# A two-layer hybrid encoder trunk: large products as one plain float32 matmul in place of three float32r matmuls on split operands

## The chip, the cores and the metric

The kernel runs on one core of one Trainium2 chip. The metric is the device time of one execution in microseconds (us), the median of several runs. TensorE (PE in the profile) multiplies matrices, VectorE (DVE), ScalarE (ACT) and GpSimd (POOL) work elementwise, and SyncE (SP) issues all DMAs of this kernel in order. PEld is TensorE's weight load.

## The reference

The input x has 512 tokens of width 1024, in float32. Two layers each do

```
x += 0.5 * SwiGLU(RMSNorm(x))            # 1024 -> 2 x 2816 -> 1024
x += W_out( sum_m sigmoid(gate_m) * P_m(mixer_m(RMSNorm(x))) )
x += 0.5 * SwiGLU(RMSNorm(x))
```

The four mixers read one common input projection of the normalised x (10520 columns): differential attention, gated linear attention (GLA), a Mamba-2 state space (SSD), and RWKV-7, which is a recurrence over the tokens. A last RMSNorm gives the output. All weights are float32 and are read once: 478 blocks ("units") of 128 x 1024 numbers, 512 KB each.

## The kernel before

**Units and products.** `unit` loads 128 x 1024 weights, copies them on ScalarE into a float32r tile `whi` and takes the rest `wlo = wraw - whi` on VectorE. (float32r is a matmul input type of four bytes and of less precision than float32.) The other operand of each large product stands as such a pair too: `xh/xl` after a norm, `hh/hl` after the gated product of a feed-forward block (FFN), `yh/yl` and `ah/al` in the merge. `mm3` then makes a product of three matmuls:

```
mm(out=ps, lhsT=lh, rhs=rh, start=first, stop=False)
mm(out=ps, lhsT=lh, rhs=rl, start=False, stop=False)
return mm(out=ps, lhsT=ll, rhs=rh, start=False, stop=last)
```

In what follows a *product* is one such step: 128 x 128 stationary numbers times 128 x 512 moving ones into one PSUM tile. A unit makes eight. `feat` makes 128 features of all tokens (eight products), `tok` makes 512 columns for four token tiles, `merge` multiplies a branch by its slice of the branch weights. `feat2` makes the first two units of an FFN or mixer with 256 moving columns at a time, because the second half of the tokens is normalised later.

**Stages.** Each layer is FFN, mixer, FFN. An FFN is 44 units of gate and up projection and 22 of the down projection. A mixer has 59 `feat` units (32 of them the gates), 24 `tok` units, 16 merge units and 8 of the output projection.

**The order in the mixer.** `cotrace` writes two streams of work, RWKV (`first`) and the three other branches (`others`), in the order of estimated times that they yield (TensorE's cost of a piece, and the latency after it). Where TensorE would idle, it puts in a piece of a `filler`: first the 32 gate units, then the merges. Merges come only after RWKV and attention are done. A scheduler in the framework then orders the instructions of each engine; each engine runs its list in order.

RWKV's chain per half of its heads is: projections and preparation; a triangular inverse on VectorE of 62 small instructions (tiles `itmp` and `xi`), which goes through DRAM before and after (`nx<-nd`, `xdi<-xi`) and ends in the matmuls of lines 705 and 709; then eight chunks in turn, each a chain of matmuls (lines 735, 743, 749, and 759 and 762 for the output) with small VectorE work between; then the store of the branch. Narrow matmuls of the mixers (transposes, attention, chunks) take plain float32 operands already.

Of the kernel before, what the change touches and what calls it, by code (L numbers as in the profile page):

```python
# [11 lines left out]
F32R = mybir.dt.float32r  # L12
# [61 lines left out]
class Body:  # L74
# [4 lines left out]
    # ---------------------------------------------------------------- helpers  # L79
# [22 lines left out]
    def rsqrt(self, y, a, pool, tag):  # L102
        """y = a ** -0.5 for normal positive a."""
# [14 lines left out]
    def rsqrt_neg_half(self, hm, pool):  # L118
        """a ** -0.5 for the [128, 1] tile hm = -a / 2."""
# [3 lines left out]
        # the shifted sign and the halved exponent are in the constant  # L123
# [38 lines left out]
    def mm3(self, ps, lh, ll, rh, rl, first, last):  # L162
        mm = self.nc.tensor.matmul
        mm(out=ps, lhsT=lh, rhs=rh, start=first, stop=False)  # L164
        mm(out=ps, lhsT=lh, rhs=rl, start=False, stop=False)  # L165
        return mm(out=ps, lhsT=ll, rhs=rh, start=False, stop=last)  # L166

    def feat(self, ap):
        """[128 features, 512 tokens] of the projection by one unit."""
        hi, low = self.unit(ap)  # L170
        ps = self.small("pb")
        for k in range(8):
            c = slice(k * 128, (k + 1) * 128)
            self.mm3(ps, hi[:, c], low[:, c], self.xh[:, k, :], self.xl[:, k, :], k == 0, k == 7)
        return ps

    def feat2(self, aps):
        """Two units' projections, the first half of the tokens before the second."""
        ws = [self.unit(ap, "pool") for ap in aps]
        pss = [self.small("pb") for _ in aps]  # L180
        last = None
        for h in range(2):
            n = slice(256 * h, 256 * h + 256)
            for (hi, low), ps in zip(ws, pss):
                for k in range(8):
                    c = slice(k * 128, (k + 1) * 128)
                    last = self.chained(last if k == 0 else None, lambda: self.mm3(
                        ps[:, n], hi[:, c], low[:, c], self.xh[:, k, n], self.xl[:, k, n], k == 0, k == 7))
        return pss

    def tok(self, units, lh, ll, tags=("pb", "pb", "oy", "oy"), tail=0):
        """Four [128 tokens, 512] products: stationary lh/ll (feature-major), moving the units.
        The last tail units go by token tile, so that the tiles end one after another."""
        mm = self.nc.tensor.matmul
# [3 lines left out]
        def one(t, k, hi, low):  # L198
            lt = slice(t * 128, (t + 1) * 128)
            c = slice((k % 2) * 512, (k % 2 + 1) * 512)  # L200
            mm(out=pst[t], lhsT=lh(k)[:, lt], rhs=hi[:, c], start=k == 0, stop=False)  # L201
            mm(out=pst[t], lhsT=lh(k)[:, lt], rhs=low[:, c], start=False, stop=False)  # L202
            mm(out=pst[t], lhsT=ll(k)[:, lt], rhs=hi[:, c], start=False, stop=k == nk - 1)  # L203

        n = len(units) - tail
        for u, ap in enumerate(units[:n]):
            w = self.unit(ap)
            for k in (2 * u, 2 * u + 1):
                for t in range(NT):
                    one(t, k, *w)  # L210
        ws = [self.unit(ap) for ap in units[n:]]
        for t in range(NT):
            for j, w in enumerate(ws):
                for k in (2 * (n + j), 2 * (n + j) + 1):
                    one(t, k, *w)
# [5 lines left out]
    # ------------------------------------------------------------------ norm  # L221
# [9 lines left out]
    def norm_(self, x, gain, pool, out=None, g=None):  # L231
        """RMS norm of x (tiles [t][half]); to xh/xl feature-major, or rows to out."""
        nc = self.nc
        if out is None:
            self.xh = self.xp.tile([128, 8, 512], F32R, tag="xh", name="xh")
            self.xl = self.xp.tile([128, 8, 512], F32R, tag="xl", name="xl")
        if g is None:
            g = self.gain_row(gain, pool)
        for t in range(NT):
            # hm = -(mean square + eps) / 2, the first half's part ahead of the second's  # L240
# [8 lines left out]
            for h in range(2):  # L249
# [8 lines left out]
                nc.scalar.copy(self.xh[o], ps)  # L258
                self.sub(self.xl[o], ps, self.xh[o].bitcast(F32))
# [1082 lines left out]
```

## Time and profile before

| | |
|---|---|
| median of 3 runs | 3218.39 us (3214.93 to 3223.4) |
| span of the profiled execution | 3212.2 us |
| PE busy | 3147.8 us |
| DVE busy | 1621.3 us |
| ACT busy | 1148.1 us |
| moved by DMA | 338.50 MB, mean 105 GB/s |

The profiled execution is listed with its span only; the median of the runs lies 6.2 us (0.2%) above it. Busy time of PE is a sum over overlapping matmuls, whose ends are modelled, so the rate of the matmuls is read from their starts.

### The profile page before, as it was taken

The page shows a single profiled execution, that of the slowest core. Times are in us where ns is not written, and L with a number is a line of the kernel's source. Part 1 is how long each engine was busy: PE and PEld are TensorE (multiplying, and loading weights), DVE is VectorE, ACT ScalarE, POOL GpSimd, SP SyncE. Part 2 cuts the span into 40 slices and gives each one's busy share as a digit, 9 for nine tenths or more (in the row PEclk, how much of TensorE's full clock was granted, in tenths as well). Part 3 has the DMA queues.
Part 4 walks back from the last instruction along what each step waited for, and adds up shares of the span by engine and source line. Part 5 has one row for each costly group of instructions (what it writes and reads, how often), then busy time and mean ns, then how long its engine had stood idle before and what let it go on. Part 6 is the DMA issues. An engine that isn't in the chain of part 4 may idle for free.

```text
span 3212.2 us, 40884 instructions
## 1 busy us (share of the span) xinstructions
PE 3147.8 (98%) x16160; PEld 2499.3 (78%) x16160; DVE 1621.3 (50%) x3310; ACT 1148.1 (36%) x1754; POOL 137.8 (4%) x160
## 2 busy tenths in 40 slices
PE   8999999999999999999999999999999999999998
PEld 6888787777777777888888888777777777778887
DVE  4332446756475775332343324567654757753323
ACT  3222245654432323222222223356553323232222
POOL 0000000000011100000000000000000011000000
PEclk9999999999999999999999999999999999999999
DMA  4222322322222543222332233223122215432222
GB/s 165 98 98 93 129 89 88 103 67 96 86 83 63 180 168 138 99 98 93 108 132 94 99 112 110 93 87 104 60 93 95 86 56 181 172 132 93 98 99 79
DMA packets 138592, 338.50 MB, mean 105 GB/s; under 512 B 35104, under 2 KB 43680, under 8 KB 137632
## 3 DMA queue, kind: packets, MB, share of 16 engines
q1 hardware_dynamic: 138400, 335.88, 30.8%
q8 instruction: 127, 2.08, 0.3%
q14 instruction: 65, 0.53, 0.1%
HBM read 297.55 MB, written 38.27 MB: 105 GB/s over the span
## 4 chain that ended last, share of the span: by engine, by line
PE 90%; DVE 7%; ACT 2%; issue 1%; DMA 0%; SPq 0%; DVEq 0%; ACTq 0%
PE pb L164 18%; PE pb L165 18%; PE pb L166 18%; PE oy L203 3%; PE oy L201 3%; PE oy L202 3%; PE pb L202 2%; PE pb L201 2%; PE pb L203 2%; PE rs L203 1%; PE os L203 1%; PE rs L201 1%; PE os L201 1%; PE os L202 1%; PE rs L202 1%; PE os L871 1%
## 5 line engine op out<-in xcount | busy, mean ns | idle before, releaser
L157 ACT CAST whi<-wraw 128x1024 fp32r<-128x1024 f32 x478 | 501.6, 1051 | 1479.6 <-PE pb L165 545.8
L159 DVE TENSOR_TENSOR wlo<-wraw,whi 128x1024 fp32r<-128x1024 f32 x466 | 571.7, 1227 | 894.5 <-ACT whi L157 880.8
L164 PE MATMUL pb<-xh,whi 128*128 128x512 f32 (+1 forms) x2448 | 957.0, 391 | 4.9 <-DVE rwr L97 2.7
L165 PE MATMUL pb<-xl,whi 128*128 128x512 f32 (+1 forms) x2448 | 949.5, 388 | 3.4 <-DVE xl L81 3.4
L166 PE MATMUL pb<-xh,wlo 128*128 128x512 f32 (+1 forms) x2448 | 949.6, 388 | 0.0
L164 PEld LDWEIGHTS pb<-xh,whi 128*128 128x128 f32 x2448 | 466.5, 191 | 110.2 <-issue 16.6
L165 PEld LDWEIGHTS pb<-xl,whi 128*128 128x128 f32 x2448 | 466.7, 191 | 95.8 <-issue 6.3
L166 PEld LDWEIGHTS pb<-xh,wlo 128*128 128x128 f32 x2448 | 467.0, 191 | 93.5 <-issue 6.1
L81 DVE TENSOR_TENSOR s<-s,pb 128x512 f32<-128x512 f32 x88 | 60.5, 688 | 286.9 <-PE pb L166 284.8
L100 ACT ACT_TABLE_LOAD x118 | 151.4, 1283 | 12.5 <-PE os L1141 9.7
L165 PE MATMUL pb<-yl,whi 128*128 128x512 f32 x256 | 102.1, 399 | 0.9 <-DVE yl L81 0.9
L164 PE MATMUL pb<-yh,whi 128*128 128x512 f32 x256 | 102.5, 403 | 0.0
L166 PE MATMUL pb<-yh,wlo 128*128 128x512 f32 x256 | 102.1, 399 | 0.0
L159 POOL TENSOR_TENSOR wlo<-wraw,whi 128x1024 fp32r<-128x1024 f32 x12 | 28.4, 2379 | 1318.3 <-ACT whi L157 1318.3
L202 PE MATMUL pb<-wlo,xh 128*128 128x512 f32 x192 | 76.7, 399 | 0.0
L201 PE MATMUL pb<-whi,xh 128*128 128x512 f32 x192 | 76.6, 399 | 0.0
L201 PE MATMUL oy<-whi,xh 128*128 128x512 f32 x192 | 76.0, 396 | 0.0
L203 PE MATMUL oy<-whi,xl 128*128 128x512 f32 x192 | 75.8, 395 | 0.0
L203 PE MATMUL pb<-whi,xl 128*128 128x512 f32 x192 | 75.8, 395 | 0.0
L202 PE MATMUL oy<-wlo,xh 128*128 128x512 f32 x192 | 75.3, 392 | 0.0
L201 PE MATMUL pb<-whi,hh 128*128 128x512 f32 x176 | 69.1, 392 | 0.0
L202 PE MATMUL pb<-wlo,hh 128*128 128x512 f32 x176 | 69.0, 392 | 0.0
(418 smaller groups left out, 4339.7 us busy)
## 6 DMA issues: line engine op xcount, KB each, us to landing
wraw<-in_ffn_gu SPq DMA_DIRECT2D x176, 512.0 KB, 3.2
wraw<-in_win_f SPq DMA_DIRECT2D x118, 512.0 KB, 3.3
wraw<-in_ffn_d SPq DMA_DIRECT2D x88, 512.0 KB, 3.2
wraw<-in_win_t SPq DMA_DIRECT2D x48, 512.0 KB, 3.3
gd<-sg SPq DMA_DIRECT2D x64, 256.0 KB, 2.1
wraw<-in_wbr SPq DMA_DIRECT2D x32, 512.0 KB, 3.4
msg<-gd SPq DMA_DIRECT2D x64, 256.0 KB, 3.0
wraw<-in_wout SPq DMA_DIRECT2D x16, 512.0 KB, 3.2
```

The costliest lines, as they stand in the source:

```text
L81: return (eng or self.nc.vector).tensor_tensor(out=out, in0=in0, in1=in1, op=op)
L100: return self.nc.scalar.activation(out=out, in_=in_, func=func, **kw)
L157: nc.scalar.copy(hi, raw)
L159: eng.tensor_tensor(out=low, in0=raw, in1=hi.bitcast(F32), op=ALU.subtract)
L164: mm(out=ps, lhsT=lh, rhs=rh, start=first, stop=False)
L165: mm(out=ps, lhsT=lh, rhs=rl, start=False, stop=False)
L166: return mm(out=ps, lhsT=ll, rhs=rh, start=False, stop=last)
L201: mm(out=pst[t], lhsT=lh(k)[:, lt], rhs=hi[:, c], start=k == 0, stop=False)
L202: mm(out=pst[t], lhsT=lh(k)[:, lt], rhs=low[:, c], start=False, stop=False)
L203: mm(out=pst[t], lhsT=ll(k)[:, lt], rhs=hi[:, c], start=False, stop=k == nk - 1)
L871: mm(out=s[:, 0:n], lhsT=qT[qb][cp_, h, :], rhs=kT[h][cp_, 0:n], start=True, stop=True)
```

## The change

The split is taken out everywhere. A unit is used as it was loaded, the other operands are single float32 tiles (`xT`, `hT`, `y`, the merged `acc`), and each product is one matmul on float32 operands. The casts to float32r and the subtractions go, on weights and on the other operands. Two smaller sums that used float32r pairs (RWKV's `bones` product and the SSD's `gtbd` product) become one float32 matmul each. The weight pool has 8 buffers of one tile instead of 3 of three. `cotrace`'s estimate of a `feat` unit goes from 5.2 to 3.5 and of a `tok` group from 20.8 to 14.0, so the order of the mixer is another one. Comments were dropped.

```diff
-    def unit(self, ap, lo="dve"):
-        nc = self.nc
-        raw = self.wp.tile([128, 1024], F32, tag="wraw", name="wraw")
-        nc.sync.dma_start(out=raw, in_=ap)
-        hi = self.wp.tile([128, 1024], F32R, tag="whi", name="whi")
-        low = self.wp.tile([128, 1024], F32R, tag="wlo", name="wlo")
-        nc.scalar.copy(hi, raw)
-        eng = nc.gpsimd if lo == "pool" else nc.vector
-        eng.tensor_tensor(out=low, in0=raw, in1=hi.bitcast(F32), op=ALU.subtract)
-        return hi, low
+    def unit(self, ap):
+        w = self.wp.tile([128, 1024], F32, tag="w", name="w")
+        self.nc.sync.dma_start(out=w, in_=ap)
+        return w
...
-            self.mm3(ps, hi[:, c], low[:, c], self.xh[:, k, :], self.xl[:, k, :], k == 0, k == 7)
+            self.nc.tensor.matmul(out=ps, lhsT=w[:, k * 128 : (k + 1) * 128], rhs=self.xT[:, k, :],
+                                  start=k == 0, stop=k == 7)
...
-                nc.scalar.copy(self.xh[o], ps)
-                self.sub(self.xl[o], ps, self.xh[o].bitcast(F32))
+                nc.scalar.copy(self.xT[o], ps)
...
-                self.mul(s, s, psu)
-                nc.scalar.copy(hh[:, f, :], s)
-                self.sub(hl[:, f, :], s, hh[:, f, :].bitcast(F32))
+                self.mul(hT[:, f, :], s, psu)
...
-                pe += 5.2
+                pe += 3.5
...
-                mm(out=psb, lhsT=self.bones, rhs=qh, start=True, stop=False)
-                mm(out=psb, lhsT=self.bones, rhs=ql, start=False, stop=True)
+                mm(out=psb, lhsT=self.c("bones"), rhs=q, start=True, stop=True)
...
-            self.wp = ep(name="w", bufs=3)
+            self.wp = ep(name="w", bufs=8)
```

Two places in TensorE's list show what moves. The first is the start of the program, where `feat2` stands between the transposes of the first norm (`os<-ident,xn`). Before:

```order
L256 MATMUL os<-ident,xn 128x128 x16
L164 MATMUL pb<-xh,whi 128x256
L165 MATMUL pb<-xl,whi 128x256
L166 MATMUL pb<-xh,wlo 128x256
L164 MATMUL pb<-xh,whi 128x256
```

With the change, up to the end of the first gate and up projections:

```order
L239 MATMUL os<-ident,xn 128x128 x16
L174 MATMUL pb<-xT,w 128x256 x3
L239 MATMUL os<-ident,xn 128x128 x8
L174 MATMUL pb<-xT,w 128x256 x3
L239 MATMUL os<-ident,xn 128x128 x8
L174 MATMUL pb<-xT,w 128x256 x26
L160 MATMUL pb<-xT,w 128x512 x336
```

Where three matmuls stood for a product there is one, of the same columns.

The second place is the scan of RWKV's second half of heads, at its fifth chunk of eight (`rs<-st,ar` reads the state and begins a chunk, `rs<-un,tt` and `rs<-sav,bk` are its next two steps). Before, the products of an SSD projection (`pb` and `oy`, from `wlo` and `whi`) stand between the steps of the chunk:

```order
L735 MATMUL rs<-st,ar 64x64 x3
L202 MATMUL pb<-wlo,xh 128x512
L203 MATMUL pb<-whi,xl 128x512
L201 MATMUL oy<-whi,xh 128x512
L202 MATMUL oy<-wlo,xh 128x512
L743 MATMUL rs<-un,tt 64x64 x4
L203 MATMUL oy<-whi,xl 128x512
L201 MATMUL oy<-whi,xh 128x512
L202 MATMUL oy<-wlo,xh 128x512
L203 MATMUL oy<-whi,xl 128x512
L749 MATMUL rs<-sav,bk 64x64 x4
```

With the change the same chunk steps (now lines 693, 701 and 707) have only narrow matmuls of the SSD and of RWKV's output between them:

```order
L693 MATMUL rs<-st,ar 64x64 x4
L677 MATMUL rs<-ident,yc 64x64 x4
L1077 MATMUL os<-ident,conv 128x128 x3
L701 MATMUL rs<-un,tt 64x64 x4
L1077 MATMUL os<-ident,conv 128x128
L1085 MATMUL os<-ident,conv 128x128 x2
L707 MATMUL rs<-sav,bk 64x64 x4
```

The products that stood here have moved ahead in the list, and from this chunk to the first merge none is left.

## Rows read from the trace of the kernel before

**Rows 1.** The page: span, busy time by engine, TensorE's granted clock in 40 slices.
```profile
span 3212.2 us, 40884 instructions
PE 3147.8 (98%) x16160; PEld 2499.3 (78%) x16160; DVE 1621.3 (50%) x3310; ACT 1148.1 (36%) x1754; POOL 137.8 (4%) x160
PEclk9999999999999999999999999999999999999999
```
**Rows 2.** Stretches by window: the first layer's mixer; 100 us inside an FFN.
```profile
370.00:1235.00 865.00, 852.38 (x4826) 648.66 (x4825) 551.55 (x1328) 372.61 (x617) 60.07 (x75) 0.99 0.31 104
...
100.00:200.00 100.00, 100.00 (x442) 82.78 (x442) 35.27 (x38) 29.88 (x38) 0.00 (x0) 1.00 0.27 95
```
**Rows 3.** Waits on TensorE: engine, tile, line, who ended them, us in total.
```profile
PE os L256 <- DVE xn L97: 35.0, 18, 10.3
PE pb L165 <- DVE xl L81: 3.4, 5, 2.1
```
**Rows 4.** The page's groups: the casts of the units to float32r.
```profile
L157 ACT CAST whi<-wraw 128x1024 fp32r<-128x1024 f32 x478 | 501.6, 1051 | 1479.6 <-PE pb L165 545.8
```
**Rows 5.** Groups by shape on TensorE: a plain float32 matmul of full size.
```profile
L793 PE MATMUL rs<-rwg,lor 128*128 128x512 f32 x16 | 8.6, 618 | 0.0
```
**Rows 6.** Timeline on TensorE where line 793 stands between float32r products.
```profile
1060.83 1.02 PE L793 MATMUL rs<-rwg,lor 128*128 128x512 f32 x2
1061.28 0.80 PE L164 MATMUL pb<-xh,whi 128*128 128x512 f32 x1
1061.92 0.40 PE L165 MATMUL pb<-xl,whi 128*128 128x512 f32 x1
1062.15 0.39 PE L166 MATMUL pb<-xh,wlo 128*128 128x512 f32 x1
```
**Rows 7.** Timeline on TensorE: a plain float32 matmul with narrow neighbours.
```profile
2307.79 1.12 PE L948 MATMUL os<-misc,lor 16*128 16x512 f32 x2
2308.84 0.45 PE L719 MATMUL rs<-ident,yc 64*64 64x64 f32 x8
```
**Rows 8.** VectorE's groups from 903 to 973 us, RWKV's second inverse.
```profile
L97 DVE SCALAR_TENSOR_TENSOR conv<-pb,prm,conv 128x509 f32<-128x509 f32 (+2 forms) x18 | 13.3, 738 | 5.7 <-ACT conv L100 5.5
L81 DVE TENSOR_TENSOR xi<-xi,itmp 64x31 f32<-64x31 f32 (+15 forms) x31 | 13.0, 418 | 0.3
L159 DVE TENSOR_TENSOR wlo<-wraw,whi 128x1024 fp32r<-128x1024 f32 x9 | 11.0, 1219 | 1.1 <-ACT whi L157 1.0
L81 DVE TENSOR_TENSOR itmp<-nx,xi 64x31 f32<-64x31 f32 (+15 forms) x31 | 10.2, 330 | 0.2
```
**Rows 9.** TensorE's groups in the same stretch, one of the three lines of a product.
```profile
L166 PE MATMUL pb<-xh,wlo 128*128 128x512 f32 x73 | 29.6, 405 | 0.0
```
**Rows 10.** Timeline: start of the inverse (SP) and first matmul behind it (PE).
```profile
901.06 0.50 SPq L660 DMA_DIRECT2D nx<-nd  x1
...
973.64 0.69 PE L705 MATMUL rs<-xt,am 32*32 32x32 f32 x16
```
**Rows 11.** Timeline: two chunks of the first scan; fifth chunk of the second; load for the merge.
```profile
653.12 0.45 PE L749 MATMUL rs<-sav,bk 128*64 128x64 f32 x8
...
657.55 0.45 PE L749 MATMUL rs<-sav,bk 128*64 128x64 f32 x8
...
1011.73 0.33 PE L735 MATMUL rs<-st,ar 64*64 64x64 f32 x2
...
1064.19 0.43 SPq L382 DMA_DIRECT2D y<-yd  x1
```
**Rows 12.** TensorE's groups from 1012 to 1070 us: the scan's output matmuls.
```profile
L759 PE MATMUL rs<-sav,am 128*64 128x64 f32 x40 | 6.6, 246 | 0.0
L762 PE MATMUL rs<-st,ar 64*64 64x64 f32 x40 | 6.5, 242 | 0.0
```
**Rows 13.** DMA issues: KB each, median us from issue to landing.
```profile
y<-yd SPq DMA_DIRECT2D x6, 1024.0 KB, 5.3
wraw<-in_win_f SPq DMA_DIRECT2D x118, 512.0 KB, 3.3
```

More of the change, by code (lines that the diff above doesn't have):

```diff
@@ L11 @@
 F32 = mybir.dt.float32
-F32R = mybir.dt.float32r
 I32 = mybir.dt.int32
@@ L148, in chained @@
             return fn()
-    def unit(self, ap, lo="dve"):
-        nc = self.nc
-        raw = self.wp.tile([128, 1024], F32, tag="wraw", name="wraw")
-        nc.sync.dma_start(out=raw, in_=ap)
-        hi = self.wp.tile([128, 1024], F32R, tag="whi", name="whi")
-        low = self.wp.tile([128, 1024], F32R, tag="wlo", name="wlo")
-        nc.scalar.copy(hi, raw)
-        eng = nc.gpsimd if lo == "pool" else nc.vector
-        eng.tensor_tensor(out=low, in0=raw, in1=hi.bitcast(F32), op=ALU.subtract)
-        return hi, low
[L162 to L166, printed above, removed]
+    def unit(self, ap):
+        w = self.wp.tile([128, 1024], F32, tag="w", name="w")
+        self.nc.sync.dma_start(out=w, in_=ap)
+        return w
     def feat(self, ap):
-        hi, low = self.unit(ap)
+        w = self.unit(ap)
         ps = self.small("pb")
         for k in range(8):
-            c = slice(k * 128, (k + 1) * 128)
-            self.mm3(ps, hi[:, c], low[:, c], self.xh[:, k, :], self.xl[:, k, :], k == 0, k == 7)
+            self.nc.tensor.matmul(out=ps, lhsT=w[:, k * 128 : (k + 1) * 128], rhs=self.xT[:, k, :],
+                                  start=k == 0, stop=k == 7)
         return ps
     def feat2(self, aps):
-        ws = [self.unit(ap, "pool") for ap in aps]
+        ws = [self.unit(ap) for ap in aps]
         pss = [self.small("pb") for _ in aps]
@@ L183, in feat2, with tok, one @@
             n = slice(256 * h, 256 * h + 256)
-            for (hi, low), ps in zip(ws, pss):
+            for w, ps in zip(ws, pss):
                 for k in range(8):
                     c = slice(k * 128, (k + 1) * 128)
-                    last = self.chained(last if k == 0 else None, lambda: self.mm3(
-                        ps[:, n], hi[:, c], low[:, c], self.xh[:, k, n], self.xl[:, k, n], k == 0, k == 7))
-        return pss
-    def tok(self, units, lh, ll, tags=("pb", "pb", "oy", "oy"), tail=0):
-        mm = self.nc.tensor.matmul
+                    last = self.chained(last if k == 0 else None, lambda: self.nc.tensor.matmul(
+                        out=ps[:, n], lhsT=w[:, c], rhs=self.xT[:, k, n], start=k == 0, stop=k == 7))
+        return pss
+    def tok(self, units, lh, tags=("pb", "pb", "oy", "oy"), tail=0):
         pst = [self.small(t) for t in tags]
         nk = 2 * len(units)
[L198 to L203, printed above, removed]
+        def one(t, k, w):
+            self.nc.tensor.matmul(
+                out=pst[t], lhsT=lh(k)[:, t * 128 : (t + 1) * 128],
+                rhs=w[:, (k % 2) * 512 : (k % 2 + 1) * 512], start=k == 0, stop=k == nk - 1)
         n = len(units) - tail
@@ L209, in tok @@
                 for t in range(NT):
-                    one(t, k, *w)
+                    one(t, k, w)
         ws = [self.unit(ap) for ap in units[n:]]
@@ L214, in tok @@
                 for k in (2 * (n + j), 2 * (n + j) + 1):
-                    one(t, k, *w)
+                    one(t, k, w)
         return pst
@@ L298, in ffn @@
                 units = [a["ffn_d"][i, h, j] for j in range(11)]
-                pst = self.tok(units, lambda k: hh[:, k, :], lambda k: hl[:, k, :], TAGS[h], tail=TAIL * h)
+                pst = self.tok(units, lambda k: hT[:, k, :], TAGS[h], tail=TAIL * h)
                 for t in range(NT):
@@ L345, in mix @@
                 x = self.load_x(xsrc, yp, "x")
-                acc = []
-                for _ in self.merge(2, self.yc, gd, yp, acc):
+                for _ in self.merge(2, self.yc, gd):
                     pass
@@ L350, in mix @@
                     units = [a["wout"][l, h, u] for u in range(4)]
[L351 to L352 removed]
+                    pst = self.tok(units, lambda k: self.acc[k], TAGS[h], tail=TAIL * h)
                     for t in range(NT):
@@ L401, in filler @@
                 yield True
-    def y_split(self):
-        return [self.mp.tile([128, 4, 512], F32R, tag=t, bufs=2, name=t) for t in ("yh", "yl")]
     def gate(self, gd, i):
@@ L442, in merge @@
         for u in range(4):
-            hi, low = self.unit(a["wbr"][self.l, m, u])
+            w = self.unit(a["wbr"][self.l, m, u])
             for d2 in range(2):
@@ L450, in merge @@
                     c = slice((d2 * 4 + k) * 128, (d2 * 4 + k + 1) * 128)
-                    self.mm3(ps, hi[:, c], low[:, c], yh[:, k, :], yl[:, k, :], k == 0, k == 3)
+                    nc.tensor.matmul(out=ps, lhsT=w[:, c], rhs=y[:, k, :], start=k == 0, stop=k == 3)
                 if first:
@@ L458, in merge @@
                 self.add(acc[d], acc[d], sg)
-                if outs is not None:
-                    if d % 4 == 0:
-                        outs.append([lp.tile([128, 4, 512], F32R, name=n) for n in ("ah", "al")] if d else self.y_split())
-                    nc.scalar.copy(outs[-1][0][:, d % 4, :], acc[d])
-                    self.sub(outs[-1][1][:, d % 4, :], acc[d], outs[-1][0][:, d % 4, :].bitcast(F32))
-            yield 5.2, 0
+            yield 3.5, 0
     def rwkv(self, ydst):
@@ L1134, in ssd @@
             pl = self.small("os", (128, 512))
-            for j in range(2):
-                rr = self.g2((128, 8, 64), F32R, name="rr")
-                self.mul(
-                    rr, das[j][:, t, :].unsqueeze(2).to_broadcast([128, 8, 64]),
-                    self.c("tri").unsqueeze(1).to_broadcast([128, 8, 64]), nc.vector if j else nc.gpsimd,
-                )
-                mm(out=pl, lhsT=self.gtbd, rhs=rr.rearrange("p h i -> p (h i)"), start=j == 0, stop=j == 1)
+            rr = self.g2((128, 8, 64), name="rr")
+            self.mul(
+                rr, da[:, t, :].unsqueeze(2).to_broadcast([128, 8, 64]),
+                self.c("tri").unsqueeze(1).to_broadcast([128, 8, 64]), nc.gpsimd,
+            )
+            mm(out=pl, lhsT=self.c("gtbd"), rhs=rr.rearrange("p h i -> p (h i)"), start=True, stop=True)
             xe = self.g2((128, 8, 64), name="xe")
```

81 lines of the change are left out of this document (30 added, 51 removed).

## Prediction, made before the change was run

> **What bounds the kernel now.** I read the page first. TensorE is busy for 98% of the span and at its full granted clock, VectorE for 50%, ScalarE for 36% [rows 1]. Busy time of a pipelined engine can deceive, so the next view is the stretches: inside an FFN 442 matmuls start in 100 us and the clock is 1.00 [rows 2], which is one every 0.226 us, without a hole. A product of three float32r matmuls takes 0.679 us of TensorE there. In the mixer TensorE is busy for 852 of 865 us [rows 2]. The list of waits ends the question: the longest wait of TensorE is on the norms' VectorE chain and sums to 35 us in the whole run [rows 3]. So this is a TensorE-bound kernel; work on the other engines is nearly all hidden, and what the change does to the time is what it does to TensorE's list.
>
> **What is removed beside TensorE.** All 478 units lose a cast of 1.05 us on ScalarE [rows 4] and a subtraction of 1.2 us on VectorE (nine of them stand in the stretch of [rows 8]). TensorE does not wait for them, so I cost this at nothing: the eight products of the unit before, 5.4 us, hide the 2.3 us of a split, as three buffers of each tile let it run ahead. Without that cover the splits would be worth up to 478 x 2.3 us, but no row shows TensorE waiting for `whi` or `wlo`. One wait of TensorE was on an `xl` subtraction, 3.4 us in all [rows 3]; with that and a shorter end of each norm I count 5 us gained.
>
> **What a product costs after the change.** The number of products follows from the units: 478 [rows 4] times 8 is 3824. Twelve units go through `feat2` (two at each of four FFNs and two mixers), so 96 of these are made in 192 halves of 256 columns; 3728 are whole.
>
> The program holds plain float32 matmuls of the same size already, so their price can be read. Line 793 is one matmul in a loop over two heads' pairs, two halves and two layers: eight in the program. The profile has 16 of them [rows 5]. So one plain float32 matmul is run as two. How long the two hold TensorE is read from starts, not from their busy time: the pair starts at 1060.83, the next float32r matmul is recorded at 1061.28 but is 0.80 us long, and the one behind it starts at 1061.92 [rows 6]. From 1060.83 to 1061.92 are 1.09 us; one float32r matmul of 0.23 us is in it (the next step is 1061.92 to 1062.15). The pair took 0.86 us. That is 0.43 us for each of the two, almost twice a float32r matmul. The stationary load of line 793 is a full 128 x 128 one, as in the products.
>
> So a product goes from 0.679 to 0.86 us: the change replaces three matmuls by what runs as two, each of double length, four units of time for three. 3728 x 0.18 us = 671 us. For the halves I take half of each price: 192 x 0.09 us = 17 us. The two small sums (16 places, eight each) go from two float32r matmuls, 0.45 us, to 0.86: 7 us. Together 695 us longer.
>
> Bounds of that price. Above: where a plain float32 matmul is followed by a narrow one, the pair takes from 2307.79 to 2308.84, 1.05 us [rows 7]; if every product paid that, the sum would be 3728 x 0.37 = 1380 us. Below: 0.85, if the second decimal of line 793 errs by one, which is 37 us less. I take 0.86, since products follow products, full size on full size, and line 793 between full-size neighbours is the nearest row.
>
> The Trainium skill (Perfetto Trace Analysis, section Engine Utilization) gives TensorE's peak as halved for FP32_LOW_HIGH; read as the price of a plain float32 matmul, that is, by an estimate from twice the float32r step, 0.45 us for a product. The same skill (FP8 and Floating Point Precision, section TensorE Precision Notes) says that true float32 takes four passes through the array, by an estimate from four float32r steps 0.90 us. The first would make a product shorter than three float32r matmuls, the second longer. The trace agrees with the second: 0.86 us on line 793.
>
> **What the new order in the mixer costs.** The planner counts a `feat` unit at 3.5 us; at 0.86 us a product it takes 6.9. Filler is given out for gaps as if it were cheap, so the gates run out earlier. I looked at the two places in a layer where RWKV's chain is long and TensorE's list is thin.
>
> First, the second inverse. Before, it takes from the load of `nx` at 901.06 to line 705 at 973.64 [rows 10], 72.5 us, and about 72 products stand beside it [rows 9], which is 49 us, and so some 21 us of narrow matmuls. After, the list has 17 products between line 609, the last before the inverse, and line 663, the first after it: 14.6 us, with the same narrow ones about 36 us. The chain gets shorter too: nine subtractions, 11.0 us, go, and of 18 `conv` instructions, 13.3 us [rows 8], only six stand ahead of the inverse's end in the new list of VectorE, which is 8.9 us less. 72.5 - 19.9 = 53 us of chain over 36 us of work leaves TensorE idle for about 17 us. The bounds are 0, if the chain is its own instructions alone (23.2 us [rows 8], and transfers), and 36, if nothing of it shortens.
>
> Second, the end of the second scan. From its fifth chunk on there is no product in the new list until the first merge. Before, the fifth chunk begins at 1011.73, and the load that the merge needs is issued at 1064.19 [rows 11]: 52.5 us, with 5.3 for the load [rows 13]. A chunk can take as little as 4.4 us (653.12 to 657.55 [rows 11]) where nothing is in its way; with four chunks at 5.5 and a tail cut by 3 us I expect about 42 us in all. The narrow matmuls in it are at least 13 us (lines 759 and 762 [rows 12]), and with the SSD's perhaps 30. Idle: 12 to 29 us; I take 16.
>
> Elsewhere products twice as long as planned keep TensorE ahead of its streams: the first inverse has 46 products beside it, 39 us. Idle time together 33 us a layer, 66 us for two.
>
> **The sum.** 3212 + 695 + 66 - 5 = 3968 us of span. The profiled span lies 6 us under the median, and the second decimals of the prices are rounded upwards (0.429 a matmul is as good a reading as 0.43, and takes 8 us off). I predict 3965 us.
>
> Transfers don't bind: a unit's load takes 3.3 us from issue to landing [rows 13], TensorE now needs one every 6.9 instead of 5.4 us, and eight buffers stand for it.
>
> **The rivals.**
> *Faster.* A plain float32 matmul in a stream costs one matmul's 0.43 us and not two, because line 793's second record is something else. Place: every product. Then 3728 x 0.25 us and half as much on the halves, some 950 us, are saved, the mixers fall back on their chains (about 50 us a layer), and the time is about 2370 us. It decides as soon as a product is under 0.68 us. The planner's 3.5 us a unit fits it; the 16 records for eight matmuls and the 1.09 us of [rows 6] speak against. 4%. (The skill's halved peak, above, says the same; no row bears it out.)
> *Stationary loads show.* Two matmuls for each product also need two loads, and 1.05 us as on line 948 is paid: 3212 + 1380 + some = 4600 us. The pair of line 793 speaks against it, and PEld is busy for 78% beside PE already, hidden [rows 1]. 3%.
> *The chains take more.* Idle time at both places at its upper bound, and some at the first inverse: 36 + 29 + 15 a layer instead of 33, 4060 us. 12%.
> *Relief.* VectorE and ScalarE lose their splits, chains get so short that TensorE never waits: the 66 us are not paid, and 10 of today's waits go: 3895 us. 14%.
> *No change* would need a product of 0.68 us, which no row is near: 1%.
>
> **How the numbers follow.** The forecast has 66%. The range reaches from the relief to the chains' case, 3880 to 4065 us, and leaves out the first two rivals and what else I haven't thought of. Differences under 0.3% (10 us) can't be told from none here. Slower has 0.95, faster 0.04, same 0.01.
>
> **What would show it.** In the profile after, matmuls of `feat` on `xT` and `w` appear 16 to a unit, and in an FFN about 233 of them start in 100 us (0.43 us each), at full clock. The FFN stages get longer by 27%, each by some 93 us. ScalarE has no casts of weights. TensorE's waits list the `rs` tiles of the inverse (line 663) and of the chunks, at 20 to 60 us a layer. The prediction is wrong in its main step if the starts in the FFN are 0.22 us apart (faster) or over 0.5 us (loads show), and in its second if the mixers grow by much less or more than 155 + 33 us each.

## The result, and the profile after

| | before | after |
|---|---|---|
| median | 3218.14 us (3214.93 to 3223.4, 4 runs) | 3914.61 us (3914.18 to 3915.89, 4 runs) |
| span of the profiled execution | 3212.2 us | 3913.1 us |
| ratio of the medians | | 1.2169, interval 1.2151 to 1.2186 |
| PE busy, and matmul records | 3147.8 us, 16160 | 3824.7 us, 12240 |
| DVE busy, ACT busy | 1621.3, 1148.1 us | 939.3, 582.6 us |

The kernel is slower by 22%. The forecast was 3965 us in a range from 3880 to 4065.

The page after, to be held against [rows 1]:

```profile
span 3913.1 us, 31239 instructions
PE 3824.7 (98%) x12240; PEld 1822.3 (47%) x12240; DVE 939.3 (24%) x2660; ACT 582.6 (15%) x1136; POOL 95.1 (2%) x148
PEclk9999999999989799999999999999999898999999
```

TensorE is busy for the same 98% of a longer span. VectorE and ScalarE lost 682 and 566 us of work, and the time went the other way. New is that the clock row has slices under 9, at the same place in both layers.

The costliest groups by shape on TensorE, and four stretches by window (PE busy and its matmuls in brackets, then PEld, DVE, ACT and POOL, the mean granted clock, the DMA share and GB/s). They answer to [rows 2] and [rows 5]:

```profile
L160 PE MATMUL pb<-xT,w 128*128 128x512 f32 x4512 | 2007.6, 598 | 9.3 <-issue 8.8 <-DVE rwv L96 0.4
```
```profile
100.00:200.00 100.00, 100.00 (x234) 44.27 (x233) 5.50 (x8) 4.18 (x7) 0.00 (x0) 1.00 0.23 75
483.00:1510.00 1027.00, 993.22 (x3882) 490.01 (x3881) 397.55 (x1145) 238.91 (x467) 46.75 (x70) 0.96 0.27 86
1117.30:1180.10 62.80, 47.26 (x189) 25.02 (x188) 40.82 (x135) 10.46 (x21) 3.48 (x4) 0.76 0.19 45
1258.20:1317.50 59.30, 47.52 (x323) 30.52 (x323) 33.78 (x113) 8.14 (x21) 7.12 (x9) 0.65 0.18 60
```

Line 160 has 4512 records for 2256 products: every plain float32 matmul runs as two. The first window is inside an FFN: 234 records start in 100 us, one every 0.429 us from start to start, so a product takes 0.858 us, at full clock. The other three are the first mixer, its second inverse and the end of its second scan. In these two places TensorE is not full, and the clock is down to 0.76 and 0.65 on the mean. The places by the timeline (start, duration, engine; SPq issues loads), to be held against [rows 10, 11]:

```profile
1117.32 0.50 SPq L618 DMA_DIRECT2D nx<-nd  x1
...
1180.10 0.69 PE L663 MATMUL rs<-xt,am 32*32 32x32 f32 x16
...
1258.16 0.45 PE L693 MATMUL rs<-st,ar 64*64 64x64 f32 x8
...
1309.20 0.37 SPq L355 DMA_DIRECT2D y<-yd  x1
...
1316.19 1.11 PE L1148 MATMUL os<-ident,xd 128*128 128x128 f32 x4 [6.60 <-DVE xd L93]
```

The inverse takes 62.8 us from `nx` to line 663, where it took 72.5. From the fifth chunk to the load of `y` are 51.0 us, where there were 52.5, and TensorE then waits 6.60 us before it goes on.

The longest waits of TensorE after (tile and line, who ended them, us in all, times, longest one; `issue` where the profile shows nothing that it waited for):

```profile
PE os L239 <- DVE xn L96: 13.6, 12, 10.6
PE os L1148 <- DVE xd L93: 13.2, 2, 6.6
PE oy L185 <- issue: 11.7, 2, 5.8
PE pb L160 <- issue: 8.8, 2, 4.4
PE os L1008 <- DVE og L80: 7.5, 4, 2.1
PE rs L677 <- DVE yc L80: 5.3, 2, 2.7
```

The wait on the norms' chain, 35.0 us in [rows 3], is 13.6, and 10.6 of that is the first norm of the program. The rest are waits in the mixers, once a layer or twice: before, those on `og` and `yc` came to 1.1 and 1.7 us, and the others were not there.

Time by stage, each from the last transpose of a norm to the last transpose of the next (an FFN's 371.0, 371.9, 371.7 and 365.9 us before are 460.7, 459.0, 459.0 and 457.4 after; the mixers' 850.1 and 854.0 are 1027.0 and 1027.9): the FFNs grew by 355.6 us, the mixers by 350.8 (177 and 174), and the start up to the end of the first transposes got 5.4 us shorter (27.6 to 22.2). To split a stage further I summed the time from each matmul's start to the next one's:

| us, whole program | before | after | change |
|---|---|---|---|
| products at the price of their step (0.227 and 0.429 a record) | 2598.5 | 3277.8 | +679 |
| matmuls other than products in the mixers, with their waits | 424.4 | 515.1 | +91 |
| what product steps in the mixers took beyond their price | 113.8 | 70.9 | -43 |
| the same and the transposes in the FFNs | 47.9 | 27.1 | -21 |
| start, up to the end of the first transposes | 27.6 | 22.2 | -5 |

The columns add up to the spans, and the changes to their 701 us.

### The profile page after: what moved, and what is told of

It is laid out like the page before. It is cut to its first block, busy times and chain, and to the rows that moved or that the text cites. A ratio compares the mean times of both kernels' runs of the same rounds, so it can differ in the third digit from the quotient of the medians.

```text
span 3913.1 us, 31239 instructions
## 1 busy us (share of the span) xinstructions
PE 3824.7 (98%) x12240; PEld 1822.3 (47%) x12240; DVE 939.3 (24%) x2660; ACT 582.6 (15%) x1136; POOL 95.1 (2%) x148
## 4 chain that ended last, share of the span: by engine, by line
PE 93%; DVE 4%; ACT 1%; issue 1%; DMA 0%; SPq 0%; DVEq 0%; ACTq 0%
PE pb L160 48%; PE oy L185 8%; PE pb L185 8%; PE pb L418 6%; PE rs L185 5%; PE os L185 5%; PE pb L174 2%; PE rs L717 1%; PE rs L720 1%; PE os L239 1%; PE rs L573 1%; PE os L829 1%; PE oy L983 1%; PE os L989 1%; DVE itmp L80 1%
## 5 line engine op out<-in xcount | busy, mean ns | idle before, releaser
L160 PE MATMUL pb<-xT,w 128*128 128x512 f32 x4512 | 2007.6, 598 | 9.3 <-issue 8.8
L160 PEld LDWEIGHTS pb<-xT,w 128*128 128x128 f32 x4512 | 839.2, 191 | 992.2 <-issue 976.9
L99 ACT ACTIVATE s<-pb 128x512 f32<-128x512 f32 x88 | 52.5, 597 | 1109.4 <-PE pb L160 1089.8
L185 PE MATMUL oy<-w,xT 128*128 128x512 f32 x384 | 186.0, 603 | 11.7 <-issue 11.7
L185 PE MATMUL pb<-w,xT 128*128 128x512 f32 x384 | 181.8, 595 | 0.0
L418 PE MATMUL pb<-y,w 128*128 128x512 f32 x384 | 171.2, 602 | 0.0
L185 PE MATMUL rs<-w,hT 128*128 128x512 f32 x352 | 165.4, 592 | 0.0
L185 PE MATMUL os<-w,hT 128*128 128x512 f32 x352 | 165.4, 592 | 0.0
L185 PE MATMUL pb<-w,hT 128*128 128x512 f32 x352 | 163.1, 592 | 0.0
L185 PE MATMUL oy<-w,hT 128*128 128x512 f32 x352 | 162.6, 592 | 0.0
L174 PE MATMUL pb<-xT,w 128*128 128x256 f32 x384 | 86.5, 383 | 0.0
```

The source lines that it names most:

```text
L99: return self.nc.scalar.activation(out=out, in_=in_, func=func, **kw)
L160: self.nc.tensor.matmul(out=ps, lhsT=w[:, k * 128 : (k + 1) * 128], rhs=self.xT[:, k, :], start=k == 0, stop=k == 7)
L174: last = self.chained(last if k == 0 else None, lambda: self.nc.tensor.matmul(out=ps[:, n], lhsT=w[:, c], rhs=self.xT[:, k, n], start=k == ...
L185: self.nc.tensor.matmul(out=pst[t], lhsT=lh(k)[:, t * 128 : (t + 1) * 128], rhs=w[:, (k % 2) * 512 : (k % 2 + 1) * 512], start=k == 0, sto ...
L418: nc.tensor.matmul(out=ps, lhsT=w[:, c], rhs=y[:, k, :], start=k == 0, stop=k == 3)
```

## The experiments

The changed kernel's 3914.6 us is the measure for the variants of it, 3218 us for those of the kernel before; every ratio is to runs of the kernel before on the same chip. Those took 3212 to 3217 us on the median, so a difference of under some 10 us is read from the stages of the traces and not from the time.

**Plain products in the feed-forward blocks alone, and in the mixers alone.** Both start from the kernel before, with its three weight tiles of three buffers; a flag chooses the kind of product (`False, True` in the second).

```diff
+PF, PM = True, False  # plain float32 products in the feed-forward blocks, in the mixers
...
+        if self.plain:
+            return raw, None
...
+        if self.plain:
+            return mm(out=ps, lhsT=lh, rhs=rh, start=first, stop=last)
...
-                self.sub(self.xl[o], ps, self.xh[o].bitcast(F32))
+                if not plain:
+                    self.sub(self.xl[o], ps, self.xh[o].bitcast(F32))
```

> The kernel before with plain float32 products in the four feed-forward blocks alone; the mixers keep their split products, their order and the planner's prices. Theory (the price of a product is 0.858 us wherever it stands, nothing else in a feed-forward block binds): each block grows by 88 to 90 us as it did in the full change, the mixers stay at 850 and 854 us, and the time is 3218 + 4 x 89 = 3574 us (3560 to 3590). Rival (part of the growth belongs to the full change's eight weight buffers, or to engines freed all over the program): the blocks grow by over 95 or under 83 us, and the time lies outside 3550 to 3600.

> The kernel before with plain float32 products in the two mixers alone, the planner's prices left at 5.2 a unit (20.8 a group, 10.4 and 5.6 for the attention's projections); the feed-forward blocks keep their split. The SSD's gtbd sum and RWKV's bones sum keep their float32r pairs. Theory (the idle stretches of the full change's mixers come from the price 3.5 by which the planner gives filler away too early): with 5.2 the mixers grow by the products' 151 us each and little more, 3218 + 2 x 155 = 3528 us (3510 to 3545). Rival (the idle comes from longer products on the chains, whatever the price): they grow by 175 us each as in the full change, 3568 us (3555 to 3585).

FFNs alone: 3563.1 us, ratio 1.107 (1.106 to 1.109), 346 us more; by stages the blocks take 464.0, 459.5, 462.3 and 457.7 us, 87.6 to 93.0 more than before, and the mixers stay at 849.7 and 849.9. The first theory holds in the main, and three buffers of a tile do as well as eight. Inside an FFN the windows view reads as in the full change:

```profile
100.00:200.00 100.00, 100.00 (x234) 44.27 (x233) 5.49 (x8) 4.18 (x7) 0.00 (x0) 1.00 0.25 75
```

Mixers alone: 3461.0 us, ratio 1.076 (1.074 to 1.078), below both ranges, on the first theory's side. A mixer takes 980.7 and 980.9 us, 130.6 and 126.9 more than before, while its products alone take 151.5 more (582.9 to 734.4 us). With the planner's old prices the mixers do not only lose the idle stretches; what lies around the products gets shorter by over 20 us each. The first mixer by window:

```profile
393.00:1374.00 981.00, 971.46 (x3895) 478.76 (x3894) 406.84 (x1163) 250.32 (x482) 52.21 (x70) 0.99 0.30 91
```

TensorE is without work for 9.5 us there, 33.8 in the changed kernel (1027.00 - 993.22). In the sum of the two runs, 346 + 244 = 590 us, 106 us of the full change's 696 are missing: that much hung on its order in the mixers and on what the two halves do to each other. The FFN stages of the second run also tell of the norms: those whose norm feeds a mixer, and so plain products, take 364.8 and 364.6 us, and the one whose norm feeds split products 373.3.

**The planner's prices.** The changed kernel with the prices of before, and with prices that fit the products' measured time.

```diff
-                pe += 3.5
+                pe += 5.2
...
-            yield 3.5, 0
+            yield 5.2, 0
```

The first has 5.2, 20.8, 10.4 and 5.6 at all places, the second 6.9, 27.5, 13.8 and 7.3.

> The changed kernel with the planner's prices of before (5.2 a unit, 20.8 a group, 10.4 and 5.6) in place of 3.5, 14.0, 7.0 and 3.9; nothing else. In TensorE's list 42 products stand between RWKV's second preparation and the matmuls behind the second inverse, where the changed kernel has 17. Theory (the idle stretches come from the price): the second inverse is covered, the end of the second scan in part, 20 to 35 us a layer less than 3914.6: 3855 us (3840 to 3880), and no stretch of 20 us at a lowered clock at the second inverse. Rival (the chains are as long as before whatever stands beside them, what is gained at the inverse is lost at the scan's end): 3905 to 3920 us.

> The changed kernel with the planner's prices set to what the products take in its trace (6.9 a unit, 27.5 a group, 13.8 and 7.3). 47 products stand beside the second inverse, and the products between the chunks of both scans are spread thinner. Theory (idle comes from the price): 3845 us (3830 to 3875), at or a little under the run with 5.2. Rival (idle is not a matter of the price): 3905 to 3920 us. A third outcome, slower than with 5.2, would say that filler saved for the end of the second scan matters more than filler at the inverses.

With the old prices: 3822.5 us, ratio 1.189 (1.187 to 1.190), 92 us less than the changed kernel and more than expected. With the fitted ones: 3847.6 us, 1.196 (1.194 to 1.198), 67 us less, so the third outcome holds: the right price is not the best one. What the expectation takes that to say of filler at the scan's end was not tested. The page, the mixer and the second inverse by window, and two waits, of the run with 5.2:

```profile
span 3820.4 us, 31267 instructions
PEclk9999999999999999999999999999999999999999
```
```profile
482.00:1464.00 982.00, 974.77 (x3879) 476.80 (x3877) 395.83 (x1145) 244.30 (x471) 47.18 (x72) 1.00 0.28 90
1068.00:1123.90 55.90, 55.90 (x211) 26.80 (x209) 36.15 (x125) 11.46 (x19) 1.26 (x1) 0.97 0.32 88
```
```profile
PE os L239 <- DVE xn L96: 13.3, 8, 11.0
PE rs L717 <- DVE st L96: 4.1, 2, 2.0
```

The second inverse is full of matmuls, and the mixer has 7.2 us without work in place of 33.8. The waits on `issue` and on `xd` are gone. That is 26.6 us a mixer of the 44.6 that the first one gained (1027.0 to 982.4). The other 18 us are in no wait. What differs besides is the clock: of the changed kernel's mixers 61 and 66 us of TensorE's work lie in stretches of half clock, of this one's 7 and 3.

**One place at a time.** What the half clock costs, and whether the two places that the prediction named are the whole of it, is asked by holding gate units back from the planner and writing them at one place. Four gates at the last chunks of the second scan, then eight:

```diff
+                while n >= 28 and not self.late:
+                    yield False
+                n += 1
                 self.gate(gd, m * 8 + d)
...
+                if ph == 1 and c >= 4:  # the last 4 gates stand between these chunks' steps
+                    self.late = True
+                    for _ in range(1):
+                        next(self.fill)
+                    self.late = False
```

> The changed kernel with four gate units in each layer (32 products, 27 us) held back from the planner and written one to a chunk between the steps of the last four chunks of RWKV's second scan. The list around both inverses keeps its products within a few. It asks what the product-free stretch at the scan's end costs: in the changed kernel's trace TensorE waits 11.8 us between 1255 and 1320 us, and its clock is at the half level for 37.5 us there. Theory A (the half clock costs as well as the waits: narrow matmuls take about twice as long there, and products between them keep the clock up): 20 to 28 us a layer, 3914.6 - 48 = 3866 us (3855 to 3878), and no half-clock stretch of over 10 us at the scan's end. Theory B (the waits alone cost, the narrow matmuls are hidden in the chain): at most 11.8 us a layer, 3891 to 3910 us.

> The same with eight gate units held back, two to a chunk: 64 products, 55 us, more than the stretch is long. Theory A: no more is to be had at the scan's end than with four, and what is taken away beside the first half's chunks may begin to show: 3860 to 3880 us. Theory B: 3891 to 3915 us.

Four gates: 3899.4 us, ratio 1.214 (1.212 to 1.216). Eight: 3894.4 us, 1.212 (1.210 to 1.214). Both times lie in theory B's ranges, but its mechanism doesn't hold. Eight gates gave 3.9 us more than four by the mixers' stages (1016.5 and 1017.0 us after 1019.3 and 1018.1). The mixer of the run with four, by window:

```profile
483.00:1500.00 1017.00, 984.64 (x3870) 481.43 (x3869) 398.18 (x1144) 232.43 (x461) 47.16 (x70) 0.97 0.27 86
```

TensorE is without work for 32.4 us of it, as long as before the edit (33.8); the 6.6 us on `xd` are still there. What fell is the work at half clock, from 61 and 66 us a mixer to 43 and 39 (its longest stretch at the scan's end is 10.2 us in place of 37.5), and the stages got 7.7 and 9.8 us shorter. So theory A's mechanism fits, at a smaller price, if what is left beside the idle is put down to the clock: 6.4 us (the 1.3 us of idle taken off) for 17.9 us, 10.5 for 27.1, over a third. The changed kernel's own trace shows that it is not half. Two steps of the scan's output at the one and at the other clock, and the stretches that they stand in:

```profile
1267.57 0.32 PE L720 MATMUL rs<-st,ar 64*64 64x64 f32 x2
...
1268.08 0.33 PE L720 MATMUL rs<-st,ar 64*64 64x64 f32 x2
...
1279.19 0.47 PE L720 MATMUL rs<-st,ar 64*64 64x64 f32 x2
...
1280.00 0.47 PE L720 MATMUL rs<-st,ar 64*64 64x64 f32 x2
```
```profile
1262.00:1268.00 6.00, 5.31 (x58) 3.57 (x56) 3.22 (x10) 0.90 (x3) 1.42 (x3) 1.00 0.01 3
1272.00:1306.00 34.00, 30.03 (x155) 18.43 (x156) 18.87 (x68) 3.39 (x10) 3.12 (x3) 0.50 0.00 0
```

The step is 0.51 us at full clock and 0.81 at half: 0.30 of 0.81 us, 37%, is the clock's. The Trainium skill (TensorE: Matmul & The Clock Gate, section HAM oscillation) reckons the extra time as half of the time at the low clock; for these 64-column matmuls the measured share is smaller.

Then four gates at the second inverse, and both places together:

```diff
+            if ph == 1:  # 4 of the last 8 gates stand beside this inverse
+                self.put(4)
             yield 0, 22.1
```

> The changed kernel with four gate units a layer held back and written where the second inverse begins: 37 products stand beside it in place of 17. In the changed kernel's trace the stretch from nx to the first matmul behind the inverse is 62.8 us long with 42.2 us of matmuls in it, so TensorE is idle for 20.6 us, and about 17 us of its narrow work runs at the half clock. Theory (idle costs its time in full, work at the half clock about a third of its time, which is what the run with gates at the scan's end gave: 22.5 us less of it in a mixer, 7.6 us a layer gained): 17 us of idle and 6 us of clock a layer, 3914.6 - 46 = 3869 us (3858 to 3882). Rival (the chain is stretched by what stands beside it, or the place that the gates leave becomes as idle): 3895 to 3915 us.

> Both places: four gates beside the second inverse and one at each of the last four chunks of the second scan, in each layer. Theory (the two places add up and make up most of what the planner's right price gains): 3914.6 - 46 - 15 = 3854 us (3840 to 3868). If the two places with all they cost were the whole loss of the new order, it would come to the 3822 us of the run with the planner's prices of before; if what eight gates leave uncovered costs as much as they give, to 3895 us or more.

At the inverse: 3873.6 us, ratio 1.205 (1.203 to 1.207), 41 us less, where 46 were expected. Both: 3852.5 us, 1.197 (1.195 to 1.199), 62 us less, where 61 were. The inverse of the first, and the first mixer of the second by window:

```profile
1096.10:1144.10 48.00, 47.75 (x168) 21.22 (x168) 33.62 (x110) 6.54 (x11) 0.00 (x0) 1.00 0.33 95
```
```profile
483.00:1500.00 1017.00, 999.90 (x3953) 493.42 (x3952) 398.43 (x1148) 231.58 (x462) 47.69 (x70) 0.99 0.28 91
```

The stretch is full, and 48.0 us long in place of 62.8. (The expectation's 42.2 us of matmuls were counted by starts; the window has 47.26 us busy, 15.5 without work.) The window of both, which reaches beyond the end of that mixer, has 17.1 us without work. So the two places add up and are two thirds of the 92 us that the price was worth. The other 30 us, 15 a layer, were not tested apart; 10 of the 15 are time without work (17.1 us to the 7.2 with the old prices).

**The end of a norm.** One more VectorE step in the way of the products.

```diff
                 nc.scalar.copy(self.xT[o], ps)
+                self.ts(self.xT[o], self.xT[o], 1.0, ALU.mult)
```

> The changed kernel with one more VectorE step in each norm: after ScalarE's copy into xT, VectorE multiplies that slice by 1.0 in place, where the kernel before subtracted to make xl; the products wait for it. The borders at the norms got 7 us shorter each in the full change. Theory A (longer products cover the norm's chain): the step is covered too, 0 to 1 us a norm, 3915 to 3921 us. Theory B (the borders got shorter because the xl step was gone): it comes back with 4 to 7 us at each of the five norms inside the program, 3935 to 3950 us.

3907.5 us, ratio 1.215 (1.212 to 1.217): no slower. The step's group, and the wait on the norms' chain:

```profile
L93 DVE TENSOR_SCALAR xT<-xT 128x512 f32<-128x512 f32 x48 | 20.5, 427 | 21.6 <-ACT xT L241 21.6
```
```profile
PE os L239 <- DVE xn L96: 14.6, 17, 10.8
```

Theory B falls: 48 steps of 0.43 us more and the FFN stages between norms are 459.3 us, as they were (459.0). (The time lies 8 us under theory A's range too: the mixers' stages were 1.4 and 7.5 us shorter in this run, which stays open.) The missing `xl` step didn't make the borders shorter.

Cover by longer products, theory A, isn't what shortened them either. The trace of the kernel before shows a third cause. The subtractions of the twelve units of `feat2` stand on GpSimd (the `eng` line of `unit`), two at each norm; only the other 466 are on VectorE. At the norm between the layers:

```profile
1605.88 4.66 POOL L159 TENSOR_TENSOR wlo<-wraw,whi 128x1024 fp32r<-128x1024 f32 x2 [367.05 <-ACT whi L157]
...
1605.99 2.27 DVE L97 SCALAR_TENSOR_TENSOR nry<-nrt,nry 128x1 f32<-128x1 f32 x1
1608.29 3.46 DVE L97 SCALAR_TENSOR_TENSOR xn<-x,nry,grow 128x512 f32<-128x512 f32 x2
...
1611.23 1.09 PE L256 MATMUL os<-ident,xn 128*128 128x128 f32 x4 [4.16 <-DVE xn L97]
```

While GpSimd subtracts, a step of the norm's VectorE chain that takes 0.16 us elsewhere takes 2.27, the two `xn` steps behind it take 3.46 in place of 1.42, and TensorE waits 4.16 us for them. The same stands at all five norms inside the program: waits of 4.0 to 4.2 us, 20.5 in all, and after the change, without these subtractions, none of them. The run with plain mixers tells the causes apart. Its norms in front of a mixer have the three-matmul products of before ahead of the same transposes, but no split behind them, and TensorE goes on without a wait (first line); its norm between the layers still has GpSimd's two subtractions, and the wait (second line):

```profile
385.85 0.63 PE L267 MATMUL os<-ident,xn 128*128 128x128 f32 x4
...
1737.34 1.09 PE L267 MATMUL os<-ident,xn 128*128 128x128 f32 x4 [4.18 <-DVE xn L98]
```

In the run with plain FFNs, where split units follow plain products, TensorE waits for the split itself instead, 0.76 us for `whi` and 1.93 for GpSimd's `wlo`.

**Four pieces to a product.** Whether stationary loads set the price.

```diff
+        for q in range(4):
+            n = slice(128 * q, 128 * q + 128)
+            for k in range(8):
...
+                    out=ps[:, n], lhsT=w[:, k * 128 : (k + 1) * 128], rhs=self.xT[:, k, n], start=k == 0, stop=k == 7))
```

> The changed kernel with each product of the feat units in four matmuls of 128 columns (2256 products; the down projections, merges and output projections stay whole). Four times as many stationary loads for the same columns. Theory (columns set the price, loads are hidden down to this size): 8 records of 0.107 us, 0.86 us a product, 3914 to 3960 us; in the kernel before, a float32r matmul of 256 columns already starts every 0.120 us beside its load, and with that price it is 0.96 us a product and 3914 + 2256 x 0.10 = 4140 us, the upper bound of this theory. Rival (a load shows once it is longer than its matmul): the load is busy for 0.19 us, 8 x 0.19 = 1.52 us a product, 3914 + 2256 x 0.66 = 5400 us.

3987.2 us, ratio 1.238 (1.236 to 1.241), above the theory's 3960 and under its upper bound of 4140. The window inside an FFN:

```profile
100.00:200.00 100.00, 100.00 (x898) 100.00 (x897) 4.81 (x7) 4.18 (x7) 0.00 (x0) 1.00 0.22 75
```

898 records in 100 us are 0.111 us each, 0.891 a product: 0.033 more on 2256 products are 74 us, and 72.6 were measured. Loads are there four times as often, the load unit is busy all the time, and still columns set the price. Whether the 4% more is the loads beginning to show or a cost of each matmul was not told apart.

**Three bfloat16 matmuls.** The version that beats both kernels in time, with products of less precision.

```diff
-        hi = self.wp.tile([128, 1024], F32R, tag="whi", name="whi")
-        low = self.wp.tile([128, 1024], F32R, tag="wlo", name="wlo")
+        hi = self.wp.tile([128, 1024], BF, tag="whi", name="whi")
+        low = self.wp.tile([128, 1024], BF, tag="wlo", name="wlo")
```

The same at `xh/xl`, `hh/hl`, `yh/yl` and `ah/al`.

> The kernel before with its three-matmul products on bfloat16 pairs in place of float32r pairs (high part rounded to bfloat16, the rest rounded to bfloat16), so the products are of less precision; everything else as before. Theory 1 (the step of a float32r matmul, 0.227 us for 512 columns, is a little over one column per clock of 2.4 GHz, 0.213 us, and bfloat16 runs at the latter): 0.64 us a product, 3218 - 3728 x 0.04 = 3070 us (3040 to 3110). Theory 2 (both types step alike): 3218 us within 15. Theory 3 (bfloat16 is granted less clock, or VectorE's writes of two-byte tiles are slower and come into the path): over 3235 us.

3074.2 us, ratio 0.955 (0.953 to 0.956): theory 1. Inside an FFN:

```profile
100.00:200.00 100.00, 100.00 (x465) 45.34 (x464) 34.97 (x38) 29.98 (x39) 0.00 (x0) 1.00 0.30 104
```

465 start in 100 us, 0.215 us each, where 442 float32r ones did [rows 2]; a product takes 0.645 us. 3728 x (0.681 - 0.645) is 134 us, and 143 were gained. The splits stay, and those on VectorE and ScalarE stay hidden; beside GpSimd's, TensorE still waits 3.9 us at each of the five norms inside the program.

## Why the prediction was right, point by point

**The price of a product was right, and it decides.** A product runs as two records, 0.858 us in the stream where line 793 had given 0.86; three float32r matmuls are 0.681 by their median step of 0.227 where I had 0.679. The term was 695 us with halves and small sums; the products' own steps come to 679, and with the 7 us that I had reckoned for the two small sums 686. (By the starts of their matmuls the small sums took 8.8 us more, waits and work at half clock included.) The FFNs alone confirm the price by themselves.

**The FFN stages grew by 88.9 us on the mean, not 93.** The products in them did what the price says; their borders got shorter by 21 us in all, and the start by 5. The step that was mis-sized is "with that and a shorter end of each norm I count 5 us gained". I had taken from [rows 3] only the wait on `xl`. The 35 us on `xn` stand in the same rows, and 20.5 of them are the five waits beside GpSimd's subtractions; the wait after is 13.6. So what failed is the sentence that the splits cost TensorE nothing: I had put all 478 subtractions on VectorE and looked for waits on `whi` and `wlo` alone, while twelve stand on GpSimd and held up the norms' chain. Three of the five waits, 12.5 us, lie at the ends of FFNs, two in the mixers.

**The new order in the mixer: the places were right, the accounts of them in part.** At the second inverse I had 17 us of idle; the window shows 15.5. But the chain was 62.8 us and not 53, and the matmuls beside it took 47 and not 36, part of them at half clock. My guess that the chain would be 20 us shorter without its neighbours on VectorE was wrong by half, and the clock, which I hadn't thought of, made up for it. Nor is the idle where I had it. Not one of TensorE's waits there is at line 663, as I had expected: 10.2 us stand in front of products that were still in its list. The profile names nothing that they waited for (`issue`), but each wait ends about 0.1 us after VectorE has read a PSUM tile of the product's name:

```profile
1145.94 0.69 DVE L80 TENSOR_TENSOR gsq<-oy,gr 128x512 f32<-128x512 f32 x1
...
1146.74 2.04 PE L185 MATMUL oy<-w,xT 128*128 128x512 f32 x2 [5.83 <-issue]
...
1159.57 0.73 DVE L96 SCALAR_TENSOR_TENSOR conv<-pb,prm,conv 128x511 f32<-128x511 f32 x1
...
1160.40 6.08 PE L160 MATMUL pb<-xT,w 128*128 128x512 f32 x10 [4.42 <-issue]
```

The second layer shows the same two waits and reads. They stand between the small steps of the inverse on VectorE. That a product waited for its PSUM tile fits, and was not tested. So 15.5 us beside my 17 is luck: the place is right, and the sum of chain less work is not how it came about.

At the scan's end I had 42 us for the last four chunks; from 1258.16 to the load of `y` at 1309.20 are 51. I had 16 us of idle; the waits of this place are 11.8 us, 6.6 of them on `xd` beside the load. What I had not in the sum is that the narrow matmuls, left almost without products between them, ran at half clock here. The matmuls other than products grew by 91 us in the two mixers, 7 of them the small sums; my 66 us of idle stand against 84. A mixer's time without work went from 12.6 us (865.00 less 852.38 in [rows 2], nearly the same stretch) to 33.8, so the idle that the change added is 21 us a mixer, not 33; by the share of a fifth to two fifths that the runs gave (below), 45 to 50 us more work at half clock is 9 to 20 us on top of it.

**The relief came too, beside the idle.** I had set it as a rival: shorter chains, and 10 us of waits gone. In the traces it stands together with the idle: what product steps in the mixers take beyond their price fell by 43 us. It shows alone where the mixers are plain and the order is that of the old prices: they then grow by 129 us, less than their products. I had not put any of it into the forecast. Eight of the 43 us are the waits beside GpSimd at the two norms that end a mixer. Which part of the rest comes from fewer changes between products and narrow matmuls, which from VectorE's shorter queue, was not told apart.

So the span's miss of 55 us (3968 to 3913) is 9 us of price, 18 the other way in the mixers' narrow work, and 64 us that borders and edges gave beyond the 5 that I had (69: 43 in the mixers' product steps, 21 in the FFNs, 5 at the start). The main step holds, and two small terms were off; the 18 us hid a part of the 64.

**The rivals.** One record a product (2370 us) and loads that show (4600 us) are out: 4512 records for 2256 products, 0.429 us each, and pieces of 128 columns cost 0.111. The chains' upper bound was not reached.

**What the order cost.** The planner's price was lowered with the change while the product got longer. Put back, it gives 92 of the 696 us; 604 us are left: the products' price less what got shorter around them. No order that was tried went below that.

## What to carry to other kernels

Count the time of a matmul in the records that the profile has for it: a plain float32 matmul that already stands in the program, between neighbours of full size, gave the price of 478 units of work to the second digit before one of them was run. When TensorE is the bound, taking over 1200 us of work off the other engines buys little: at most 69 us here, against 686 for the products, and the part whose cause is shown came from twelve subtractions on GpSimd. To trade three matmuls of 0.227 us for one of 0.858 loses. And when the price of a product changes, a planner's numbers are part of the change: try several, since the fitted ones were not the best here.

## What the hardware showed that I had not expected

The clock: in the product-free stretch at the end of the second scan TensorE was busy for 30.0 of 34 us (1272 to 1306) and was still granted 0.50, 1.2 GHz; before it fell, at 1269, the engine had run narrow matmuls from 1258 on, and one of 512 columns among them (line 1094, 1263.81). With products of full size between the same narrow matmuls (the run with the prices of before) the mean clock of the mixer is 1.00. Work at half clock cost a fifth to two fifths of its time, if what the mixer gained beyond the idle is all the clock's: 18.0 us beyond the idle for 54.5 us less of it in the first mixer with the prices of before, 10.2 for 47.6 with the fitted ones, 6.4 for 17.9 with four gates.

GpSimd and VectorE: while GpSimd ran its subtractions of 128 x 1024 (2.3 us each), a VectorE step of 0.16 us took 2.2 to 2.3, at each of the five norms inside the program.

The types: 512 columns take 0.215 us in bfloat16, 0.227 in float32r, and two times 0.429 in float32. So plain float32 takes as long as four of the bfloat16 steps (0.858 / 0.215), and the float32r step is 5% longer than the bfloat16 one. The Trainium skill (FP8 and Floating Point Precision, section TensorE Precision Notes) gives true float32 four passes through the array; the trace agrees.
